# Zero matmuls, half-opened units and a reordered weight split at the start of an encoder layer, and a later place for the sums of w_out

## The chip, the core and the metric

The kernel runs on one core of a Trainium2 chip. The metric is the device time of one execution in microseconds (us). TensorE (PE) multiplies, with its weight loads shown as PEld; VectorE (DVE), ScalarE (ACT) and GpSimd (POOL) do elementwise work, and SyncE (SP) issues nearly all DMAs. Each engine works through its own queue in order and waits on semaphores for the others.

## The reference, cut to what matters

One encoder layer over 1024 tokens of width 1024, in float32:

```python
x = LN0(alpha*x + 0.5*SwiGLU_1(x))        # first feed-forward, width 2816
u = x @ W_in                               # then attention and a two-way SSD scan
x = LN1(alpha*x + concat(a, s) @ W_out)
x = LN2(alpha*x + 0.5*SwiGLU_2(x))        # second feed-forward
x = LN3(alpha*x + sigmoid(x @ W_g + b_g) * (p @ W_p))   # p: 1024 x 256
```

`p @ W_p` (called `e` below) depends on inputs alone, so the kernel computes it first.

## The kernel before, in words

**Products.** A float32 operand is split into a high part that TensorE takes (a cast on ACT, `split_into`) and a low part, the difference (a subtraction on DVE, `lo`, line 87). A product of two such operands is three matmuls per 128 rows of contraction: high with low, low with high, high with high (`mm3`, line 122). One PSUM tile of 128x512 takes one product; the pool `sm` (`pss`) has four such tiles, the pool `big` (`psb`) two of 128x1024.

**The beginning** (`begin`). SP issues the loads of `pT` and `we` (the transposed p and W_p, in eight 256 KB pieces, tiles `xET4h` and `xET4l`), then the identity, the transposed x (`raw`, `wr`, `h`), then the first weights of the feed-forward (`sg`, `xh11`). ACT and DVE split the eight pieces into tiles named `blk`. Sixteen *units* follow (`ple_unit`): each is one 128x512 tile of `e`, with a contraction of 256 rows in two halves, so six matmuls, and ACT copies it out of PSUM (line 632). The list `beside` says which work on x and on the first weights is written between two units: `b11`, `b21` split two quarters of x, `sum1`, `t2`, `sum4` form and split sums of x, and `left(f, i)` splits half `i` of the first weights of row block `f` (`blk<-sg`).

**The first feed-forward.** Each of 22 row blocks `f` takes seven products of twelve matmuls (a Strassen-like scheme): first two that make `sg`, then those with `T2`, `T1`, `T3`, `T4`, `B22` (`ffn_rest`), whose results DVE adds up out of PSUM (`u<-sg,sm` line 378, `u<-u,sm` lines 384 and 387, `sg<-u,sm` line 388) or ACT copies (line 381). The results go to DRAM in `h` and `sg` pieces (line 348, 352).

**The sums of w_out** (`right_sums`, for both feed-forwards). For each of eleven pairs of rows of the second weight, one step issues the stores of the last sums and the loads of the next rows (`wr`, lines 314 and 315) behind SP's queue; the next step forms four sums on DVE (lines 319 to 322). They are needed as weights only in the stage after (`ffn_strassen`, which writes the `big` tiles). `ffn_h` calls one step per row block.

**What sets the order.** PE's order is the order of the program text (`in_order`). In `begin`, ACT and DVE also keep the order of the text. Everywhere else a scheduler places the instructions of ACT, DVE, POOL and SP at build time by its own estimate. `behind(engine)` holds what it encloses behind the last instruction written so far for that engine.

Of the kernel before, what the change touches and what calls it, by code (L numbers as in the profile page):

```python
# [9 lines left out]
F32 = mybir.dt.float32  # L10
F32R = mybir.dt.float32r
BF16 = mybir.dt.bfloat16
# [6 lines left out]
P = 128  # L19
# [17 lines left out]
class Layer:  # L37
# [258 lines left out]
    def right_sums(self, c, i, wo):  # L296

        nc, V = self.nc, self.nc.vector  # L300
        pool = c.enter_context(self.tc.tile_pool(name=f"wsum{i}", bufs=1))
        to = [self.dram.tile([4, P, 512], F32, name=f"wT{i}_{q}") for q in range(NP)]
        lo, hi = slice(0, 512), slice(512, 1024)

        made = []

        def store():
            for dst, src in made:
                nc.sync.dma_start(out=dst, in_=src)
            made.clear()  # L310

        def load(q):
            w1, w2 = (pool.tile([P, D], F32, name=n) for n in ("wr1", "wr2"))
            nc.sync.dma_start(out=w1, in_=wo[2 * q])
            nc.sync.dma_start(out=w2, in_=wo[2 * q + 1])
            return w1, w2, pool.tile([P, 512], F32, name="wt2")

        def sums(q, w1, w2, t):
            V.tensor_tensor(out=w1[:, lo], in0=w1[:, hi], in1=w1[:, lo], op=ALU.subtract)
            V.tensor_tensor(out=t, in0=w2[:, hi], in1=w1[:, lo], op=ALU.subtract)  # L320
            V.tensor_tensor(out=w1[:, hi], in0=w2[:, hi], in1=w1[:, hi], op=ALU.subtract)
            V.tensor_tensor(out=w2[:, lo], in0=w2[:, lo], in1=t, op=ALU.subtract)
            for k, src in enumerate((w1[:, lo], t, w1[:, hi], w2[:, lo])):
                made.append((to[q][k], src))

        tiles = {}

        def step(n):
            q = n // 2
            if n % 2:  # L330
                return sums(q, *tiles[q])
            with self.behind(mybir.EngineType.SP):
                store()
                if q < NP:
                    tiles[q] = load(q)

        return pool, to, [lambda n=n: step(n) for n in range(2 * NP + 1)]

    def left_factors(self, i, tmp):
# [267 lines left out]
    def begin(self, pool, tmp, spare):  # L607


        nc, I = self.nc, self.I  # L610
        V, A = nc.vector, nc.scalar
# [9 lines left out]
        def loaded(src):  # L621
# [2 lines left out]
            todo.append((b, r))  # L624
            return b

        def ple_unit(i, t, n):
            c = slice((t % 4) * P, (t % 4 + 1) * P)
            o = self.pss()
            self.mm3(o, [((pT[t // 4][k][:, 0, c], pT[t // 4][k][:, 1, c]), (we[n][k][:, 0], we[n][k][:, 1])) for k in range(2)])  # L630
            e = kept[i // 4][:, i % 4]
            A.copy(out=e, in_=o)
            with self.behind(mybir.EngineType.SP):
                nc.sync.dma_start(out=self.eD[t][:, n * 512:(n + 1) * 512], in_=e)

        pT, we = [[], []], [[], []]
# [15 lines left out]
        for k in range(4):  # L652
            for src in (I["xT"][:, k], I["xT"][:, k + 4]):
                i = len(raws)
# [13 lines left out]
        u1 = tmp.tile([P, S], F32, name="sg")  # L668
        nc.sync.dma_start(out=u1, in_=I["wi1"][1, 1])
        (r11, r12), (r21, r22) = ([[r[j] for r in raws[i::2]] for j in range(2)] for i in range(2))  # L670
        s = [tmp.tile([P, 512], F32, name=f"s{k + 1}") for k in range(4)]

        for b, r in todo:
            self.split_into(b, r)
# [7 lines left out]
        def put(name, k, src):  # L682
            return lambda: self.put(X, name, k, a, src)

        def less(out, x, y):
            return lambda: V.tensor_tensor(out=out, in0=x, in1=y, op=ALU.subtract)
# [3 lines left out]
        def left(f, i):  # L690
            def do():
                w[f, i] = self.split(sg[f][:, i * 512:(i + 1) * 512])
            return do

        def sum1(k):
            return [less(r11[k], r12[k], r11[k]), less(s[k], r22[k], r11[k])]
# [5 lines left out]
        def b11(k):  # L702
            return [put("B11", k, r11[k])]

        def b21(k):
            return [put("B21", k, r21[k])]

        def t2(k):
            return [put("T2", k, s[k])]

        def sum4(k):
            return [less(r21[k], r21[k], s[k])]


        beside = [[], b11(0) + b21(0), [], b11(1) + b21(1) + sum1(0), [], b11(2) + b21(2) + sum1(1), b11(3) + b21(3) + sum1(2), sum1(3),
                  t2(0) + sum4(0), t2(1) + sum4(1), t2(2) + sum4(2), t2(3) + sum4(3), [left(0, 0), left(0, 1)], [left(1, 0), left(1, 1)], [], []]
        units = [(t, n) for u in range(2) for n in range(2) for t in range(u * 4, u * 4 + 4)]
        for i, ((t, n), work) in enumerate(zip(units, beside)):
            ple_unit(i, t, n)
            for do in work:  # L720
                do()
# [45 lines left out]
        left, sums, g1 = next1  # L767
# [363 lines left out]


    def attention(self, c, mixT, aside, begin):

        nc, tc = self.nc, self.tc
# [89 lines left out]
        for i in range(n + 8):  # L1225
            ps = scores(i) if i < n else None
            los = turn(i - 2) if 2 <= i < n + 2 else []
            if 6 <= i < n + 6:
                values((i - 6) // 4, (i - 6) % 4)
            if (i - 6) % 4 == 1:  # L1230
                normalise()
            if ps is not None:
                softmax(i, ps)
            if i == 1:
                begin()
            for a in los:
                self.lo(*a)
            if i >= 8 and i % 2 == 0 and aside:
                with self.behind(mybir.EngineType.Activation), self.behind(mybir.EngineType.DVE):
                    aside.pop(0)()  # L1240
# [292 lines left out]
    def run(self):  # L1533
# [37 lines left out]
        with ExitStack() as c:  # L1571
            self.in_proj(c, xT)
            rctx.close()
            with self.behind(mybir.EngineType.SP):
                tabs = self.ssd_tables(tables)
            blocks0, aside = [], []

            def begin():
                self.z_last(xT, aside)
                early = [self.ring_raw(I["wm"][k]) for k in range(4)]  # L1580
                aside.extend(tabs)
                aside.extend(lambda i=i, r=r: blocks0.append(self.split(r[:, i * 512:(i + 1) * 512], eng=nc.gpsimd)) for i in range(2) for r in early)

            mixT = [[self.unit(h, 0)] for h in range(2)]
            with ExitStack() as c2:
                self.attention(c2, mixT, aside, begin)
# [396 lines left out]
```

## Time and profile before

| what | value |
|---|---|
| time, median of 3 runs | 1947.11 us (1946.96 to 1948.23) |
| time of the profiled execution | 1948.74 us |
| its span, first to last instruction | 1946.9 us |
| PE busy | 1927.9 us, 99% of the span |
| DVE busy | 1528.0 us, 78% |
| ACT busy | 881.1 us, 45% |
| first matmul starts | 6.75 us |
| the sixteen units end, the first product of the feed-forward starts | 31.25 us |
| first matmul of the stage after the first feed-forward's rows | 450.1 us |

In the lists of instructions, a row gives the start, the time taken, engine, line, operation, what is written and read, and how many equal ones follow each other; in brackets the idle time of the engine before and what ended it. In the list of waits a row gives who waited for whom, the total, how often and the longest. Matmuls overlap, so a matmul's own duration is longer than the distance to the next one.

### The profile page before, as it was taken

The numbers are of one execution on the slowest core, as the hardware profiler recorded it, in microseconds if no ns is written. First come the engines' busy times: TensorE is split into PE (matmuls) and PEld (weight loads), VectorE is DVE, ScalarE is ACT, GpSimd is POOL, SyncE is SP. The second block draws the span as 40 slices with busy tenths as digits, with TensorE's granted clock in tenths as the row PEclk, the third lists the DMA queues.
The fourth block names the chain that finished last, engine by engine and source line by source line (L and its number), as shares of the span: only waits on it lengthen the run. The fifth ranks groups of instructions, "written<-read, shape, count | busy, mean of one in ns | idle before, by whom it ended". The sixth has DMA issues, their size and how long they took to land.

```text
span 1946.9 us, 25645 instructions
## 1 busy us (share of the span) xinstructions
PE 1927.9 (99%) x9132; PEld 1607.8 (83%) x9132; DVE 1528.0 (78%) x2356; ACT 881.1 (45%) x1509; POOL 416.9 (21%) x310
## 2 busy tenths in 40 slices
PE   8999999999999999999999999999999999999998
PEld 6888888888888889888888888888888888888886
DVE  7977777767678668758998878997787787877698
ACT  6433333325444224537887876633333333443311
POOL 0144535430001032001221001013444440001011
PEclk9999999999999999999999999999999999999999
DMA  8434554549866111231002663244545439976022
GB/s 296 143 125 151 190 179 156 190 159 373 297 221 212 63 42 50 84 119 68 7 1 77 212 222 121 90 165 156 190 163 178 173 121 358 331 262 226 32 77 97
DMA packets 147713, 310.34 MB, mean 159 GB/s; under 512 B 18128, under 2 KB 30800, under 8 KB 147584
## 3 DMA queue, kind: packets, MB, share of 16 engines
q1 hardware_dynamic: 147584, 308.69, 45.4%
q8 instruction: 72, 1.18, 0.2%
q14 instruction: 57, 0.47, 0.1%
HBM read 217.21 MB, written 91.42 MB: 159 GB/s over the span
## 4 chain that ended last, share of the span: by engine, by line
PE 94%; DVE 3%; DMA 1%; ACT 1%; issue 1%; POOL 0%; SPq 0%; DVEq 0%; ACTq 0%
PE sm L122 59%; PE big L516 12%; PE sm L516 9%; PE big L122 3%; PE big L1159 3%; PE sm L1181 2%; PE sm L1196 1%; PE sm L1197 1%; DMA yd<-y 1%; DVE nm L1166 1%; DVE conv L977 1%; PE sm L1270 0%; PE big L224 0%; PE sm L224 0%; PE big L909 0%
## 5 line engine op out<-in xcount | busy, mean ns | idle before, releaser
L122 PE MATMUL sm<-xh,blk 128*128 128x512 f32 x1424 | 439.8, 389 | 0.0
L122 PEld LDWEIGHTS sm<-xh,blk 128*128 128x128 f32 x1424 | 267.3, 188 | 55.4
L122 PE MATMUL sm<-xl,blk 128*128 128x512 f32 x736 | 283.8, 389 | 0.0
L122 PE MATMUL sm<-blk,xl 128*128 128x512 f32 (+2 forms) x784 | 238.2, 371 | 0.2 <-ACT xn_t L1010 0.2
L122 PE MATMUL sm<-blk,xh 128*128 128x512 f32 (+2 forms) x584 | 203.3, 379 | 1.6 <-DVE acc L1466 1.1
L108 ACT CAST blk<-raw 128x512 fp32r<-128x512 f32 (+1 forms) x168 | 101.3, 611 | 215.0 <-PE sm L122 134.1
L87 DVE TENSOR_TENSOR blk<-s,blk 128x512 fp32r<-128x512 f32 x176 | 150.8, 861 | 35.2 <-ACT blk L108 33.2
L87 DVE TENSOR_TENSOR blk<-raw,blk 128x512 fp32r<-128x512 f32 (+1 forms) x168 | 146.5, 875 | 40.6 <-ACT blk L108 40.1
L108 ACT CAST blk<-s 128x512 fp32r<-128x512 f32 x172 | 105.7, 622 | 146.5 <-PE sm L122 118.3
L122 PEld LDWEIGHTS sm<-blk,xl 128*128 128x128 f32 x784 | 142.8, 188 | 24.2 <-ACT xn_t L1010 0.5
L122 PEld LDWEIGHTS sm<-xl,blk 128*128 128x128 f32 x736 | 138.2, 188 | 28.6
L178 POOL TENSOR_TENSOR ln_k<-ln_k,mhalf 128x1 f32<-128x1 f32 x32 | 37.4, 1173 | 579.2 <-DVE ln_k L177 563.0
L516 PE MATMUL big<-xh 128*128 128x512 f32 x576 | 138.8, 390 | 0.0
L267 POOL TENSOR_TENSOR s<-raw 128x512 f32<-128x512 f32 x34 | 55.0, 1617 | 387.2 <-DVE blk L87 381.7
L87 DVE TENSOR_TENSOR xh<-blk,xh 128x1024 fp32r<-128x1024 f32 x78 | 95.4, 1223 | 48.4 <-ACT xh L462 42.3
L462 ACT CAST xl<-blk 128x1024 fp32r<-128x1024 f32 x76 | 80.2, 1055 | 113.5 <-PE sm L516 43.7
L462 ACT CAST xh<-blk 128x1024 fp32r<-128x1024 f32 x78 | 82.3, 1055 | 108.1 <-PE big L516 49.9
L122 PEld LDWEIGHTS sm<-blk,xh 128*128 128x128 f32 x584 | 109.9, 188 | 21.3 <-DVE acc L1466 1.4
L516 PEld LDWEIGHTS big<-xh 128*128 128x128 f32 x576 | 107.8, 188 | 22.2
L87 DVE TENSOR_TENSOR xl<-blk,xl 128x1024 fp32r<-128x1024 f32 x76 | 92.7, 1220 | 41.3 <-ACT xl L462 36.7
L516 PE MATMUL big<-xl 128*128 128x512 f32 x480 | 115.8, 390 | 0.0
L122 PE MATMUL sm<-xET2h,blk 128*128 128x512 f32 x352 | 108.4, 389 | 0.0
(343 smaller groups left out, 4018.5 us busy)
## 6 DMA issues: line engine op xcount, KB each, us to landing
raw<-in_wi_dram SPq DMA_DIRECT2D x81, 512.0 KB
blk<-hS SPq DMA_DIRECT2D x154, 256.0 KB
hS<-h SPq DMA_DIRECT2D x88, 256.0 KB
wr<-in_wo_dram SPq DMA_DIRECT2D x44, 512.0 KB
blk<-wT SPq DMA_DIRECT2D x88, 256.0 KB
hS<-sg SPq DMA_DIRECT2D x66, 256.0 KB
wT<-wr SPq DMA_DIRECT2D x66, 256.0 KB
blk<-in_wo_dram SPq DMA_DIRECT2D x66, 256.0 KB
```

Source lines behind the costliest of these rows:

```text
L87: (eng or self.nc.vector).tensor_tensor(out=out, in0=full, in1=hi.bitcast(F32), op=ALU.subtract)
L108: self.nc.scalar.copy(out=b[:, 0, :n], in_=src)
L122: self.nc.tensor.matmul(ps, lhsT=a, rhs=b, start=(i == 0), stop=(i == n - 1))
L178: nc.gpsimd.tensor_tensor(out=r, in0=v, in1=self.mhalf[:, :1], op=ALU.pow)
L267: lambda: G.tensor_tensor(out=s1, in0=a21, in1=a22, op=ALU.add),
L462: A.copy(out=b[:, :, 0], in_=r)
L516: nc.tensor.matmul(ps[q], lhsT=b[:, 0, x, cut], rhs=b[:, 1, y], start=j == i == 0, stop=j == NP - 1 and i == 2)
L977: nc.vector.scalar_tensor_tensor(out=a[:, o], in0=ps[:, o.start + d - c:o.stop + d - c], scalar=cw[:, j, tap:tap + 1], in1=a[:, o], op0=AL ...
L1159: nc.tensor.matmul(ps[:, n * 512:(n + 1) * 512], lhsT=Q[:, h, q0:q0 + P], rhs=K[:, h // 4, j, n * 512:(n + 1) * 512], start=j == 0, stop=j ...
L1166: nc.vector.tensor_reduce(out=nm, in_=ps, axis=AX.X, op=ALU.max, negate=True)
L1181: nc.tensor.transpose(out=pt[:, k], in_=pr[:, kk * P:(kk + 1) * P], identity=self.ident)
L1196: nc.tensor.matmul(po, lhsT=vw, rhs=pth[k // 4][:, k % 4], start=k == 0, stop=False)
```

## The change

At the beginning, DVE fills 256 columns of the tile `s1` with zeros (128x256 float32, read as 512 columns of bf16), and PE runs fourteen matmuls over it into a tile of `big` that nobody reads. Then four units are opened together: of their first half of the contraction (`k = 0`) the high-high terms of all four, then the low-high ones, then the high-low ones. When a unit's turn comes, only its second half is left. The later units run both halves. The three terms now come in another order (high with high first). In `beside`, the split of the first two weight halves moves ahead of the third and fourth `t2`. In the first feed-forward, the four sums of w_out are held behind the last DVE instruction written so far; in the second they stay as they were.

```diff
@@ right_sums, step
             if n % 2:
-                return sums(q, *tiles[q])
+                if i:
+                    return sums(q, *tiles[q])
+                with self.behind(mybir.EngineType.DVE):
+                    return sums(q, *tiles[q])
@@ begin
+        s = [tmp.tile([P, 512], F32, name=f"s{k + 1}") for k in range(4)]
+        V.memset(s[0][:, :256], 0.0)
+        zero, o = s[0].bitcast(BF16), self.psb()[:, :512]
+        for i in range(14):
+            nc.tensor.matmul(o, lhsT=zero[:, :P], rhs=zero[:, :512], start=True, stop=True)
+
+        def ple_part(o, t, n, k, terms):
+            c = slice((t % 4) * P, (t % 4 + 1) * P)
+            for i, j in terms:
+                nc.tensor.matmul(o, lhsT=pT[t // 4][k][:, i, c], rhs=we[n][k][:, j], start=k + i + j == 0, stop=k + i == 2)
+
         def ple_unit(i, t, n):
-            c = slice((t % 4) * P, (t % 4 + 1) * P)
-            o = self.pss()
-            self.mm3(o, [((pT[t // 4][k][:, 0, c], pT[t // 4][k][:, 1, c]), (we[n][k][:, 0], we[n][k][:, 1])) for k in range(2)])
+            o = ahead[i] if i < 4 else self.pss()
+            for k in (0, 1) if i > 3 else (1,):
+                ple_part(o, t, n, k, ((0, 0), (0, 1), (1, 0)))
...
-        s = [tmp.tile([P, 512], F32, name=f"s{k + 1}") for k in range(4)]
...
         beside = [[], b11(0) + b21(0), [], b11(1) + b21(1) + sum1(0), [], b11(2) + b21(2) + sum1(1), b11(3) + b21(3) + sum1(2), sum1(3),
-                  t2(0) + sum4(0), t2(1) + sum4(1), t2(2) + sum4(2), t2(3) + sum4(3), [left(0, 0), left(0, 1)], [left(1, 0), left(1, 1)], [], []]
+                  t2(0) + sum4(0), t2(1) + sum4(1), [left(0, 0), left(0, 1)], t2(2) + sum4(2), t2(3) + sum4(3), [left(1, 0), left(1, 1)], [], []]
         units = [(t, n) for u in range(2) for n in range(2) for t in range(u * 4, u * 4 + 4)]
+        ahead = [self.pss() for t in range(4)]
+        for term in ((0, 0), (1, 0), (0, 1)):
+            for t in range(4):
+                ple_part(ahead[t], t, 0, 0, [term])
```

What stands in the queues. In the rows below, L lines are those of each kernel's own text, and numbers behind tile names only tell buffers apart.

On PE, fourteen pairs of a weight load and a matmul on `s_134`, the zeros, stand ahead of the units' 96 matmuls (`sm<-blk`), which are 96 before and now.

DVE near the end of the units, before: `xET2l<-s` are the low parts of `t2`, `blk<-sg` those of the first weights.

```order
L87 TENSOR_TENSOR xET2l<-s_181,xET2h 128x512
L686 TENSOR_TENSOR raw<-raw,s_181 128x512
L87 TENSOR_TENSOR xET2l<-s_182,xET2h 128x512
L686 TENSOR_TENSOR wr_161<-wr_161,s_182 128x512
L87 TENSOR_TENSOR xET2l<-s_183,xET2h 128x512
L686 TENSOR_TENSOR h_165<-h_165,s_183 128x512
L87 TENSOR_TENSOR blk<-sg,blk 128x512 x4
```

DVE at the same place now:

```order
L87 TENSOR_TENSOR xET2l<-s_135,xET2h 128x512
L699 TENSOR_TENSOR raw<-raw,s_135 128x512
L87 TENSOR_TENSOR blk<-sg,blk 128x512 x2
L87 TENSOR_TENSOR xET2l<-s_136,xET2h 128x512
L699 TENSOR_TENSOR wr_181<-wr_181,s_136 128x512
L87 TENSOR_TENSOR xET2l<-s_137,xET2h 128x512
L699 TENSOR_TENSOR h_185<-h_185,s_137 128x512
L87 TENSOR_TENSOR blk<-sg,blk 128x512 x2
```

The first two weight splits moved four instructions forward.

DVE in a row block of the first feed-forward, before: `wr` and `wt` are the sums of w_out, `u` and `sg` the sums out of PSUM.

```order
L290 TENSOR_TENSOR sg<-sg,sm 128x512
L87 TENSOR_TENSOR blk<-s_2024,blk 128x512
L378 TENSOR_TENSOR u_1890<-sg,sm 128x512
L87 TENSOR_TENSOR blk<-raw,blk 128x512
L87 TENSOR_TENSOR blk<-s_2025,blk 128x512
L319 TENSOR_TENSOR wr_1823<-wr_1823 128x512
L384 TENSOR_TENSOR u_1891<-u_1890,sm 128x512
L87 TENSOR_TENSOR blk<-raw,blk 128x512
L320 TENSOR_TENSOR wt_1827<-wr_1824,wr_1823 128x512
L321 TENSOR_TENSOR wr_1823<-wr_1824,wr_1823 128x512
L322 TENSOR_TENSOR wr_1824<-wr_1824,wt_1827 128x512
```

DVE, the same four sums now (they stand in the next row block):

```order
L290 TENSOR_TENSOR sg<-sg,sm 128x512
L355 TENSOR_TENSOR h_1992<-sg,h_1988 128x512
L319 TENSOR_TENSOR wr_1839<-wr_1839 128x512
L87 TENSOR_TENSOR blk<-s_2193,blk 128x512
L320 TENSOR_TENSOR wt_1843<-wr_1840,wr_1839 128x512
L321 TENSOR_TENSOR wr_1839<-wr_1840,wr_1839 128x512
L381 TENSOR_TENSOR u_2061<-sg,sm 128x512
L322 TENSOR_TENSOR wr_1840<-wr_1840,wt_1843 128x512
```

They moved from behind the block's first sum out of PSUM (line 378, now 381) in one block to ahead of it in the next. The scheduler also reordered DVE, ACT and SP here and there up to the first part of the stage of the `big` tiles; from there to the end of the program every queue stands as before.

## The prediction

> **What bounds the kernel now.** I read the page's busy times and chain first, then PE's waits, then the chain of the first 60 us, then the rows of the stretch that is edited.
>
> ```profile
> span 1946.9 us, 25645 instructions
> PE 1927.9 (99%) x9132; PEld 1607.8 (83%) x9132; DVE 1528.0 (78%) x2356; ACT 881.1 (45%) x1509; POOL 416.9 (21%) x310
> PE 94%; DVE 3%; DMA 1%; ACT 1%; issue 1%; POOL 0%; SPq 0%; DVEq 0%; ACTq 0%
> PE sm L122 <- DVE blk L87: 6.8, 1, 6.8
> PE sm L122 <- DVE acc L1466: 1.1, 1, 1.1
> ```
>
> PE is the bound nearly everywhere. Its one long wait is 6.8 us, for the first split operand; the next is 1.1 us and lies in a part that isn't touched. So what the change can win lies before and inside the units. The chain there:
>
> ```profile
> 0.72 0.40 SPq L623
> 1.17 4.16 DMA xET4h<-in_we_dram
> 5.35 0.63 ACT blk L108
> 6.00 0.70 DVE blk L87
> 6.75 53.44 PE sm L122 x223
> ```
>
> The load of W_p lands at 5.33, ACT's cast is done at 5.98, DVE's low part at 6.70, PE starts at 6.75 and does not stop any more. How fast it runs is the second reading, from PE's rows, windows and groups:
>
> ```profile
> 6.75 24.66 PE L122 MATMUL sm<-blk 128*128 128x512 f32 x96 [6.75 <-DVE blk L87]
> 31.25 0.39 PE L122 MATMUL sm<-xl,blk 128*128 128x512 f32 x1
> 33.97 0.39 PE L122 MATMUL sm<-xl,blk 128*128 128x512 f32 x1
> 6.75:11.95 5.20, 5.20 (x11) 1.00 1.04 371
> 11.95:31.25 19.30, 19.30 (x87) 1.00 1.04 406
> L122 PE MATMUL sm<-blk 128*128 128x512 f32 x11 | 5.4, 654 | 6.8 <-DVE blk L87 6.8
> ...
> L122 PE MATMUL sm<-blk 128*128 128x512 f32 x86 | 19.9, 391 | 0.0
> 9.42 1.05 PE L122 MATMUL sm<-blk 128*128 128x512 f32 x2
> 10.70 1.05 PE L122 MATMUL sm<-blk 128*128 128x512 f32 x2
> 31.25:450.12 418.87, 418.87 (x1849) 1.00 0.48 167
> ```
>
> Between 31.25 and 33.97 lie the twelve matmuls of one product: 0.2267 us each. At that pace 96 take 21.76 us, but the units take 24.50 (6.75 to 31.25). The 2.74 us are lost in the first 5.2 us: there eleven matmuls last 654 ns each, later ones 391. The rows at 9.42 and 10.70 lie three matmuls apart (two in flight span 1.05, one lasts about 0.63): 0.427 each, 1.9 times the later distance. The printed clock column says 1.00 in both windows, so the slow state is read from durations, not from that column. From 31.25 to 450.12 PE is busy in every microsecond: no edit there can win anything, it can only lose.
>
> **The zeros.** DVE starts as the other engines do, at 0.72. No row shows a DVE fill of 128x256; its bounds are the nearest rows:
>
> ```profile
> 0.76 0.10 POOL L1538 MEMSET pad<- 128x8 f32 x1
> 5.15 0.69 DVE L87 TENSOR_TENSOR blk<-xET4h,blk 128x512 fp32r<-128x512 f32 x1 [5.15 <-ACT blk L108]
> ```
>
> Half the columns of the second, 0.35, is my value, so PE starts on zeros at about 1.1 (0.9 to 1.5). If the clock needs PE to be busy for as long as before, 5.2 us, it rises at 6.3. By then 5.2 / 0.427 = 12.2 zeros are done; the other 1.8 take 0.4, at the fast pace. The zeros end at 6.71. They would end at 7.1 if all were slow.
>
> **The units.** The first four real matmuls take high parts only, ready at 5.98; the next four need the low part of `pT` (5.84, from the DVE row above), the last four the low part of `we` (6.70). So from 6.71 PE finds its data. Then 96 x 0.2267 = 21.76, and the first product starts at 28.47 in place of 31.25: **2.78 us won**. Is anything in the way that the old pace hid? ACT's queue, in the order that the change keeps:
>
> ```profile
> 10.95 0.57 ACT L632 COPY xh<-sm 128x512 f32<-128x512 f32 x1
> 13.93 0.59 ACT L632 COPY xh<-sm 128x512 f32<-128x512 f32 x1
> 19.37 0.59 ACT L632 COPY xl<-sm 128x512 f32<-128x512 f32 x1
> 20.37 0.63 ACT L247 CAST xh<-h 128x512 fp32r<-128x512 f32 x1
> ```
>
> The `sm` pool has four tiles, so unit 4 needs unit 0's copy (10.95 to 11.52) and would start at 6.71 + 24 x 0.2267 = 12.15; unit 6 needs unit 2's (done 14.52), starts at 14.87; unit 10 needs unit 6's (19.96), starts at 20.3. Unit 7's copy is behind the casts of x, which wait for DMA and may come no earlier: done by 21.5, and unit 11 starts at 21.67. All hold even if ACT gains nothing, by 0.2 us at the least.
>
> **The first weights.** The first product needs the low part of `w[0, 0]` at about 28.5.
>
> ```profile
> 30.20 2.49 DVE L87 TENSOR_TENSOR blk<-sg,blk 128x512 fp32r<-128x512 f32 x4
> ```
>
> Left behind all `t2` it would be done at 30.9, and PE would wait 2.4 us: without this edit most of the gain would be lost. Moved up by four instructions of 0.6 each, it starts at 27.8 with DVE no earlier, and is done at 28.5; what stands ahead of it on DVE is released by ACT's casts of x, which stand among the units' copies and move up with the units as far as DMA lets them. I cost the edit at 0. The second pair stays at 30.2 to 32.7 at the latest, for a product at 28.47 + 5.44 = 33.9.
>
> **The next pinch, 45 to 60 us.** DVE has hardly a gap there, and the order is new: the sum out of the `T3` product (line 384) now stands ahead of the sum for the next weight and of all four low parts of `B22`.
>
> ```profile
> 47.84 0.69 DVE L763 TENSOR_TENSOR sg<-sg,sm 128x512 f32<-128x512 f32 x1 [0.36 <-PE sm L122]
> ...
> 55.18 0.69 DVE L268 TENSOR_TENSOR s<-s,raw 128x512 f32<-128x512 f32 x1
> 55.79 1.29 DVE L87 TENSOR_TENSOR xl<-raw,xh 128x512 fp32r<-128x512 f32 x2
> 56.99 0.68 DVE L384 TENSOR_TENSOR u<-u,sm 128x512 f32<-128x512 f32 x1
> 58.79 0.69 DVE L87 TENSOR_TENSOR blk<-s,blk 128x512 fp32r<-128x512 f32 x1
> ```
>
> That sum waits until the `T3` product is done. Products follow each other by 2.72 (as above); `T3` is the ninth and ends 24.5 us after the first one's start, at 53.0 now. DVE waits for PE at 47.84, so from there it moves with PE, to 45.06; twelve instructions of 0.605 on, at 52.3, it reaches the sum, waits to 53.2, and then needs seven more instructions at 0.6 until the last low part of `B22`: 57.5. PE takes it as tenth matmul of the next product, at 53.0 + 2.0 + 2.72 = 57.7. So 0.2 us are left. I cost it at 0, and 0.5 at worst.
>
> **The sums of w_out.** DVE's waits in the first feed-forward:
>
> ```profile
> DVE wr L319 <- DMA wr<-in_wo_dram: 18.2, 11, 3.6
> ...
> DVE wt L320 <- DMA wr<-in_wo_dram: 3.6, 6, 1.0
> 209.57 0.68 DVE L322 TENSOR_TENSOR wr<-wr,wt 128x512 f32<-128x512 f32 x1
> ```
>
> DVE waits 21.8 us in all because the sums stand in its queue before their rows have landed. Placed later, that wait goes. But PE lost nothing to it (418.87 of 418.87 busy), so the gain is 0. What it adds: up to four sums (2.4 us) now stand ahead of the sum out of the `T2` product (line 378, now 381). That tile must be free three products later, 8.16 us. Even with the longest wait of before, 3.6 + 2.4 + 0.7 = 6.7. Cost 0. SP's stores of the sums follow at the same place of its queue as before and are needed only after 450 us. From the `big` stage on nothing is reordered: it shifts by what is won.
>
> **Sum.** The profiled execution has 1948.74 us with a span of 1946.9; less 2.78 they would be 1945.96 and 1944.1. The median of the runs is 1.6 below the profiled time; less 2.78 it gives **1944.3**, 0.14% faster. 0.2% (3.9 us) is about what a measurement of this kernel can tell from no change, so my likeliest case counts as the same.
>
> **Rivals.**
> - *The clock rises early* (18 in 100). If a shorter busy stretch is enough, the zeros end before 5.98 and PE waits for data alone: 6.0 + 21.76 = 27.8, 3.48 won, 1943.6. For it: nothing but that one ramp is on record. Against: it took 5.2. In the Trainium skill, "TensorE: Matmul & The Clock Gate" (section "Part 1: The HAM clock gate") says that the clock runs at half until one whole window of about 3.4 us was busy, and that this window is not tied to the kernel's start. By that rule the rise comes 3.4 to 6.8 us after the first zero, an estimate; the trace's 5.2 lies within, and its ratio of 1.9 agrees with half.
> - *Zeros don't wake the clock* (12 in 100). All fourteen run at 0.427 and end at 7.1; the real ones then have 5.2 slow us (12.2 matmuls) and 83.8 x 0.2267 = 19.0 more: 31.3. Nothing is won, 1947.2. Nothing in the trace shows what wakes the clock: the operands' values or the instructions.
> - *VectorE's new order costs PE about 1 us* (7 in 100), between 45 and 110 us where DVE is full: 1945.3.
> - *The sums of w_out stop PE* (4 in 100), the case on the slower side. If the rows land so late that DVE waits over 8.16 - 2.4 - 0.7 = 5.1 us ahead of line 381, PE stops for the rest, once per pair. One instruction's length, 0.6, ten times, makes 6.0: 1944.3 + 6.0 = 1950.3. Against: the longest wait was 3.6 with the sums standing earlier.
>
> **How the numbers follow.** The likeliest case (zeros end between 6.0 and 7.1, 2.0 to 3.4 won) has 59 in 100. The range 1943.1 to 1946.6 holds it, the early clock and VectorE's loss, with some tenths for the runs' own spread; left out are the zeros that don't wake the clock and the stopped PE, 16 in 100. Faster by over 0.2% means under 1943.2: the early clock's best runs only, 0.08. Slower by over 0.2% is the last rival, 0.04. The same: 0.88.
>
> **What would show it.** Right: PE's first matmul at about 1.1; slow matmuls (over 600 ns) among the zeros alone; the first product at about 28.5 with no gap in the units; PE busy without a break until about 447; no DVE wait for `wr`. Wrong: unit matmuls of over 600 ns (the zeros did not help), a gap ahead of the first product (weights late), a gap at 57 to 58 (`B22`), or PE waits in the row blocks (the sums).

## The result, and the profile after

| | before | after |
|---|---|---|
| median, first comparison (22 runs each) | 1948.25 us | 1944.89 us |
| median, a later comparison on one chip (21 and 11 runs) | 1947.83 us | 1945.01 us |
| profiled execution: time, span | 1948.74, 1946.9 us | 1944.84, 1943.0 us |
| first product of the feed-forward starts | 31.25 us | 28.68 us |

The ratio after to before is 0.9985 (95% interval 0.9979 to 0.9990), in the later comparison 0.9985 (0.9976 to 0.9994). The change is 0.15% faster: the intervals exclude 1, and it lies within the 0.2% that the prediction counted as the same. The forecast was 1944.3 us (0.14%).

The page of the changed kernel, first its head, then PE's rows from the start (start, duration, engine, line, operation, count, and in brackets the idle time ahead):

```profile
span 1943.0 us, 25694 instructions
PE 1930.9 (99%) x9146; PEld 1608.2 (83%) x9146; DVE 1521.0 (78%) x2357; ACT 880.9 (45%) x1509; POOL 419.7 (22%) x310
...
1.17 5.87 PE L634 MATMUL big<-s 128*128 128x512 bf16 x14 [1.17 <-DVE s L631]
6.70 22.15 PE L639 MATMUL sm<-blk 128*128 128x512 f32 x96
28.68 0.39 PE L122 MATMUL sm<-xl,blk 128*128 128x512 f32 x1
```

The one 6.8 us wait of PE has become 1.2 us, the zeros run, the units follow without a gap and take 21.98 us (6.70 to 28.68) instead of 24.50. Groups of PE's rows in the first 8 us (count, then busy time and mean ns of one): the slow matmuls are the zeros.

```profile
L634 PE MATMUL big<-s 128*128 128x512 bf16 x14 | 5.9, 609 | 1.2 <-DVE s L631 1.2
L639 PE MATMUL sm<-blk 128*128 128x512 f32 x5 | 1.5, 430 | 0.0
```

The window from the first product to the first `big` matmul, then DVE's waits for the rows of w_out in the first feed-forward (total, times, longest):

```profile
28.68:447.59 418.91, 418.91 (x1849) 1.00 0.48 171
...
DVE wr L319 <- DMA wr<-in_wo_dram: 3.1, 2, 2.5
DVE wt L320 <- DMA wr<-in_wo_dram: 1.1, 2, 0.6
```

PE is busy in all of the 418.91 us, as it was in 418.87 before. DVE's wait fell from 21.8 to 4.2 us, and PE got nothing from it. So 2.57 us were won by 28.68 us, and 2.53 are still there at 447.6. The profiled span is 3.9 us shorter, though. The other 1.3 us come from two later waits of PE, which the prediction did not have: 0.5 us near 1072 us became 0.3, and 1.1 us near 1142 us went. The last group of experiments is about the second.

### The profile page after: what moved, and what is told of

It is laid out like the page before. It is cut to its first block, busy times and chain, and to the rows that moved or that the text cites. A ratio compares the mean times of both kernels' runs of the same rounds, so it can differ in the third digit from the quotient of the medians.

```text
span 1943.0 us, 25694 instructions
## 1 busy us (share of the span) xinstructions
PE 1930.9 (99%) x9146; PEld 1608.2 (83%) x9146; DVE 1521.0 (78%) x2357; ACT 880.9 (45%) x1509; POOL 419.7 (22%) x310
## 4 chain that ended last, share of the span: by engine, by line
PE 95%; DVE 3%; ACT 1%; issue 1%; DMA 0%; POOL 0%; SPq 0%; DVEq 0%; ACTq 0%
PE sm L122 58%; PE big L519 12%; PE sm L519 9%; PE big L122 3%; PE big L1176 3%; PE sm L1198 2%; PE sm L1213 1%; PE sm L1214 1%; PE sm L639 1%; PE sm L1388 1%; PE sm L1287 1%; DVE nm L1183 1%; DVE conv L994 1%; PE sm L1298 0%; PE big L224 0%
## 5 line engine op out<-in xcount | busy, mean ns | idle before, releaser
L87 DVE TENSOR_TENSOR blk<-raw,blk 128x512 fp32r<-128x512 f32 (+1 forms) x168 | 141.1, 843 | 51.8 <-ACT blk L108 51.2
L87 DVE TENSOR_TENSOR blk<-s,blk 128x512 fp32r<-128x512 f32 x176 | 141.8, 809 | 40.6 <-ACT blk L108 38.5
L267 POOL TENSOR_TENSOR s<-raw 128x512 f32<-128x512 f32 x34 | 57.7, 1697 | 381.9 <-DVE blk L87 364.4
```

Of the source, the lines that this page charges most:

```text
L87: (eng or self.nc.vector).tensor_tensor(out=out, in0=full, in1=hi.bitcast(F32), op=ALU.subtract)
L267: lambda: G.tensor_tensor(out=s1, in0=a21, in1=a22, op=ALU.add),
```

## The experiments

Theory A: the slow stretch of TensorE's clock moves from the units to the zeros; the half-opened units and the earlier weight split only keep what that wins; the sums do nothing. Rival B: it is the early opening of the units that wins, and the zeros are not needed. Rival C: the sums' new place shortens the waits near 1072 and 1142 us. Rival D: a pause between zeros and units undoes the zeros.

One variant's ratio to before carries an interval of about 0.09% to each side, 1.75 us. The medians below therefore rank the variants only roughly; the verdicts rest on the rows of the traces.

| kernel | first product, us | median, us | against before in the same runs |
|---|---|---|---|
| no_zeros | 29.86 | 1946.52 | -1.3 |
| zeros_only | 29.43, then a wait | 1946.91 | -0.9 |
| weights_late | 28.30, then a wait | 1947.20 | -0.6 |
| units_whole | 29.22 | 1945.94 | -1.9 |
| sums_early | 28.65 | 1945.63 | -2.2 |
| sums_only | 30.87 | 1948.14 | +0.3 |
| zeros_11 | 28.37 | 1945.12 | -2.7 |
| zeros_6 | 30.70 | 1947.05 | -0.8 |
| zeros_28 | 30.86 | 1948.06 | +0.2 |
| after_again (the changed kernel) | 28.06 | 1945.01 | -2.8 |

### The zeros taken away (no_zeros)

```diff
-        V.memset(s[0][:, :256], 0.0)
-        zero, o = s[0].bitcast(BF16), self.psb()[:, :512]
-        for i in range(14):
-            nc.tensor.matmul(o, lhsT=zero[:, :P], rhs=zero[:, :512], start=True, stop=True)
```

> The changed kernel without its memset and its 14 matmuls over zeros; the half-opened units, the earlier weight split and the place of the sums stay. Theory A (the zeros move TensorE's slow stretch ahead of the units, the other edits only keep that gain): the first unit matmul starts near 6.0 us and runs at the slow spacing (0.42 us apart) to about 11.3; the first product of the weights starts near 30.2 us, 1.5 us later than the 28.68 of the changed kernel, and the whole takes about 1946.4 us where the changed kernel takes 1944.9. Rival B (opening four units on their first half is what wins, the zeros are not needed): first product near 28.7, whole within 0.3 us of the changed kernel. In both, the two later waits near 1070 and 1140 us, which were 1.3 us shorter in the changed kernel's trace, should stand as in that trace if they belong to the edits that stay.

PE's rows, and the group of the unit matmuls up to 9.5 us:

```profile
6.18 23.84 PE L635 MATMUL sm<-blk 128*128 128x512 f32 x96 [6.18 <-ACT blk L108]
29.86 0.39 PE L122 MATMUL sm<-xl,blk 128*128 128x512 f32 x1
...
L635 PE MATMUL sm<-blk 128*128 128x512 f32 x8 | 3.8, 653 | 6.2 <-ACT blk L108 6.2
```

The slow matmuls, 653 ns each, are back among the units, and the first product is 1.2 us later than with the zeros. B falls as it was put: the zeros are needed for the rest of the gain. But the kernel without them is still 1.4 us ahead of before at the first product, so the other edits win something by themselves. The units start at 6.18 instead of 6.75, on ACT's cast and not on DVE's low part. The slow stretch was also shorter than expected, which is no merit of the edits. A row merges many matmuls; their starts one by one, called single starts below, show where the distance falls from 0.427 to 0.227 us. Here that is at 10.14, 3.96 us after the first matmul, against 5.2 us in the first trace of before.

### The zeros alone, on the kernel before (zeros_only)

The edit is the block above, added to the kernel before.

> The kernel before with the memset and the 14 matmuls over zeros alone; units whole, old weight split, old place of the sums. Theory A: no slow matmul among the units; they start near 6.75 us, wait about 0.9 us for the split of a later block, and the low part of the first weights is done near 29.9 us, so the first product starts near 29.9 instead of 31.25: 1.3 us faster than before, about 1.2 us slower than the changed kernel. Rival B: first product near 31.2, whole as before within 0.3 us.

```profile
1.18 5.42 PE L631 MATMUL big<-s 128*128 128x512 bf16 x14 [1.18 <-DVE s L628]
6.86 0.96 PE L122 MATMUL sm<-blk 128*128 128x512 f32 x3 [0.27 <-DVE blk L87]
8.21 21.37 PE L122 MATMUL sm<-blk 128*128 128x512 f32 x93 [0.39 <-DVE blk L87]
29.43 0.39 PE L122 MATMUL sm<-xl,blk 128*128 128x512 f32 x1
30.14 0.73 PE L122 MATMUL sm<-xh,blk 128*128 128x512 f32 x2 [0.33 <-DVE blk L87]
```

As A expected: the units are fast, but PE now runs into DVE three times, twice for low parts of the units and once for the first weights. The second matmul of the first product follows 0.71 us after the first instead of 0.23, so 29.43 counts as 29.9. Zeros alone won about 1.35 us against the first trace of before, half of the change.

### The weight split left late (weights_late)

```diff
-                  t2(0) + sum4(0), t2(1) + sum4(1), [left(0, 0), left(0, 1)], t2(2) + sum4(2), t2(3) + sum4(3), [left(1, 0), left(1, 1)], [], []]
+                  t2(0) + sum4(0), t2(1) + sum4(1), t2(2) + sum4(2), t2(3) + sum4(3), [left(0, 0), left(0, 1)], [left(1, 0), left(1, 1)], [], []]
```

> The changed kernel with the split of the first weights back behind all four t2 sums (one list entry moved). If the place of this split matters: the units end near 28.5 us as in the changed kernel, TensorE then waits for VectorE, and the first product starts between 29.8 us (by the lengths of the VectorE rows of the changed kernel's own trace) and 30.9 us (what the prediction said): 1.1 to 2.2 us slower than the changed kernel. If it does not: first product at 28.7, no difference over 0.3 us.

PE's rows, then DVE's row of the first weights' low parts:

```profile
28.30 0.39 PE L122 MATMUL sm<-xl,blk 128*128 128x512 f32 x1
30.14 0.73 PE L122 MATMUL sm<-xh,blk 128*128 128x512 f32 x2 [1.45 <-DVE blk L87]
...
29.39 1.89 DVE L87 TENSOR_TENSOR blk<-sg,blk 128x512 fp32r<-128x512 f32 x3
```

PE stops for 1.45 us for the first weights, so the edit is needed. The size is the lower one: DVE reaches the split at 29.39, not at 30.20 as in the kernel before, because DVE's queue itself moved up with the units.

### The units whole again (units_whole)

```diff
-            o = ahead[i] if i < 4 else self.pss()
-            for k in (0, 1) if i > 3 else (1,):
+            o = self.pss()
+            for k in (0, 1):
```

The opening loop over `ahead` is left out with it.

> The changed kernel with each of the first eight units computed whole again, zeros kept. Theory A: the first unit needs the second half's split blocks, ready at 7.55 and 8.28 us in the changed kernel's trace, so TensorE idles 0.8 to 0.9 us in all among the first matmuls, and the first product starts near 29.5 us: 0.8 us slower than the changed kernel, 1.7 us faster than before. If the pause of TensorE lets its clock fall back: first product 30.5 or later. If the half-opened units do nothing: 28.7.

```profile
6.75 1.28 PE L639 MATMUL sm<-blk 128*128 128x512 f32 x4
8.22 21.16 PE L639 MATMUL sm<-blk 128*128 128x512 f32 x92 [0.18 <-DVE blk L87]
29.22 0.39 PE L122 MATMUL sm<-xl,blk 128*128 128x512 f32 x1
```

The change opens four units early, not eight as the expectation says. The first product is 0.54 us later than in the changed kernel's first trace (0.8 expected): the fifth matmul waits for a low part of the second half. The pause did not bring the clock down: 92 matmuls take 21.0 us (8.22 to 29.22), 0.228 each.

### The sums, in both directions (sums_early, sums_only)

```diff
-                if i:
-                    return sums(q, *tiles[q])
-                with self.behind(mybir.EngineType.DVE):
-                    return sums(q, *tiles[q])
+                return sums(q, *tiles[q])
```

This is sums_early, on the changed kernel; sums_only is the reverse on the kernel before.

> The changed kernel with w_out's sums back at their old place in VectorE's queue. Theory A (the sums' place costs and gains nothing): the wait of VectorE for the DMA of `wr` is back near 20 us, TensorE is busy without a gap through the first FFN product all the same, and the time is that of the changed kernel within 0.5 us. Rival C (the sums' new place is what shortened the waits of TensorE near 1070 and 1140 us): the 0.9 to 1.1 us gap near 1142 us is there, and the whole is about 1.3 us slower than the changed kernel.

> The kernel before with the sums behind VectorE's queue, and nothing else of the change. Theory A: first product at 30.5 to 31.5 us as before, no VectorE wait of 18 us for `wr`, time as before within 0.5 us. Rival C: the gap near 1142 us is gone and the whole is 1.3 us faster than before.

sums_early, DVE's wait and PE's first product; then sums_only, PE's rows:

```profile
DVE wr L319 <- DMA wr<-in_wo_dram: 20.9, 10, 4.1
...
28.65 0.39 PE L122 MATMUL sm<-xl,blk 128*128 128x512 f32 x1
```

```profile
6.90 24.13 PE L122 MATMUL sm<-blk 128*128 128x512 f32 x96 [6.90 <-DVE blk L87]
30.87 0.39 PE L122 MATMUL sm<-xl,blk 128*128 128x512 f32 x1
```

With the wait of 20.9 us back, the first product stands where it stood, and PE has no gap of over 0.25 us between it and the `big` stage. In sums_only the edit alone leaves the time as it was before (ratio 0.9999, interval 0.9990 to 1.0008). sums_early's median is 0.7 us above the changed kernel's, inside the intervals (its ratio to before is 0.9988, 0.9979 to 0.9997).

### How many zeros (zeros_11, zeros_6, zeros_28)

Each changes only the 14 of the loop.

> The changed kernel with 11 matmuls over zeros in place of 14. By the five traces so far TensorE's slow stretch lasts 3.9 to 5.5 us from its first matmul. 11 slow ones end at 1.17 + 11 x 0.427 = 5.87 us, the blocks of the first unit are ready near 6.0 to 6.2 us. Theory A: TensorE starts the units near 6.1 us, with at most 2 slow matmuls among them, first product at 28.0 to 28.5 us, time 0 to 0.6 us better than the changed kernel's. Rival D (a pause of 0.1 to 0.3 us between zeros and units starts the slow stretch anew): slow unit matmuls to 9.5 us or later, first product at 29.5 us or later, 0.8 to 2 us slower than the changed kernel.

```profile
1.17 4.88 PE L634 MATMUL big<-s 128*128 128x512 bf16 x11 [1.17 <-DVE s L631]
6.21 22.32 PE L639 MATMUL sm<-blk 128*128 128x512 f32 x96 [0.16 <-ACT blk L108]
28.37 0.39 PE L122 MATMUL sm<-xl,blk 128*128 128x512 f32 x1
```

A pause of 0.16 us between zeros and units did no harm: one slow unit matmul, then the fast pace from 6.8 us. D falls for pauses of this size. The median, 1945.12 us, is not to be told from 14 zeros.

> The changed kernel with 6 matmuls over zeros: they end near 1.17 + 6 x 0.427 = 3.73 us, and TensorE stands idle for some 2.4 us until the first blocks are ready. If the clock rises a fixed time after the first matmul, whatever follows (3.9 to 5.5 us in the traces): units fast from the start, first product near 28.1 us, as with 11. If TensorE has to be busy without a break: the slow stretch starts again with the units, 3.9 to 5.5 us long, so they run slow to 10 or 11.7 us, first product at 29.7 to 30.6 us, time like that of the changed kernel without zeros (1946.5).

```profile
1.17 2.74 PE L634 MATMUL big<-s 128*128 128x512 bf16 x6 [1.17 <-DVE s L631]
6.31 24.55 PE L639 MATMUL sm<-blk 128*128 128x512 f32 x96 [2.40 <-ACT blk L108]
30.70 0.39 PE L122 MATMUL sm<-xl,blk 128*128 128x512 f32 x1
```

Six zeros and a pause of 2.4 us win nothing on the clock. The units run at the slow pace again, by the single starts until 11.60, 5.3 us after the first of them. So it is not a fixed time after the first matmul that counts. In the Trainium skill, "TensorE: Matmul & The Clock Gate" (section "Part 1: The HAM clock gate") asks for one whole busy window of about 3.4 us. The six zeros are busy for 2.74, and the trace agrees. What lost the effect, the short burst or the pause behind it, this run can't tell apart: no run has a long burst with a long pause.

> The changed kernel with 28 matmuls over zeros in place of 14. TensorE works its queue in order, so zeros beyond the end of the slow stretch hold the units back at full speed: 9 to 13 slow ones to 5.1 to 6.7 us, the other 15 to 19 at 0.217 us each, so the units start near 9.4 to 10.0 us and the first product near 31.3 to 31.8 us: as before, 2.7 to 3.1 us slower than with 14. If the surplus is hidden behind the loads: 28.7.

```profile
1.17 8.04 PE L634 MATMUL big<-s 128*128 128x512 bf16 x28 [1.17 <-DVE s L631]
8.86 22.16 PE L639 MATMUL sm<-blk 128*128 128x512 f32 x96
30.86 0.39 PE L122 MATMUL sm<-xl,blk 128*128 128x512 f32 x1
```

Surplus zeros are paid in full: PE's queue is in order, the units start 2.16 us later than with 14 and end 2.18 us later. By the single starts the clock rose at 4.95 us in this execution, after nine slow zeros where the 14 had thirteen; the rest ran 0.216 us apart. Fourteen more at 0.216 are 3.02 us, and four fewer slow zeros save 0.84: 2.18. Nine slow zeros lie inside the expected 9 to 13, so the expected 31.3 to 31.8 us was itself too late: from 4.95, 19 zeros at 0.216 and 96 matmuls at 0.2267 give 30.8.

### The same kernels again (after_again, after_third, before_again)

> The changed kernel once more. The gap of TensorE near 1142 us was under 0.25 us in its first trace, and 0.35 to 1.15 us in most of the others. If it belongs to the edits of the change, it is missing again; if it goes with how the DMAs of y, raw and bc fall in one execution, it comes out anywhere from 0 to 1.15 us. The time is 1944.5 to 1945.5 us either way, the first product at 28.0 to 29.3 us by the length of the slow stretch (3.4 to 6.8 us).

> The changed kernel a third time, one look for the same gap: 0 if it belongs to the change, anywhere from 0 to 1.15 us if it goes with the execution.

> The kernel before once more, one look: the gap near 1143 us was 1.15 us in its first trace. If it belongs to the old order it is 1.1 to 1.2 us again; if it goes with the execution, it comes out anywhere from 0 to 1.15 us. The slow stretch of TensorE was 5.2 us there; by the traces so far it comes out anywhere from 3.9 to 5.5 us.

PE's first rows of after_again, then of after_third:

```profile
1.17 5.18 PE L634 MATMUL big<-s 128*128 128x512 bf16 x14 [1.17 <-DVE s L631]
6.01 22.21 PE L639 MATMUL sm<-blk 128*128 128x512 f32 x96
28.06 0.39 PE L122 MATMUL sm<-xl,blk 128*128 128x512 f32 x1
```

```profile
1.17 6.12 PE L634 MATMUL big<-s 128*128 128x512 bf16 x14 [1.17 <-DVE s L631]
6.77 22.31 PE L639 MATMUL sm<-blk 128*128 128x512 f32 x96
28.92 0.39 PE L122 MATMUL sm<-xl,blk 128*128 128x512 f32 x1
```

The same instructions start their first product at 28.06, 28.68 or 28.92 us. before_again has it at 31.36. after_third and before_again were one execution each, of 1946.15 and 1949.01 us. Now the late wait, in PE's waits between 1130 and 1150 us: before_again, sums_early, after_again, after_third, one row each (total, times, longest).

```profile
PE sm L122 <- DVE acc L1466: 1.2, 1, 1.2
```

```profile
PE sm L122 <- DVE acc L1480: 1.1, 1, 1.1
```

```profile
PE sm L122 <- DVE acc L1483: 0.4, 1, 0.4
```

```profile
PE sm L122 <- DVE acc L1483: 1.1, 1, 1.1
```

The changed kernel's first trace has no such row in this window. One and the same kernel shows 0, 0.4 and 1.1 us, so the 1.1 us that its first profile won there are no sure property of the change. What differs is a DMA in the chain that ends at this wait, in the first trace and in the third (start, duration):

```profile
1127.42 4.16 DMA raw<-in_wm_dram
```

```profile
1128.65 4.84 DMA raw<-in_wm_dram
```

It lands at 1131.58 and at 1133.49, 1.9 us later, though the start of the third ran only 0.24 us behind. C is not needed for the spread. It isn't ruled out for the mean: the four traces with the sums at their old place have 1.0 to 1.2 us, the ten with the new place 0 to 1.1, on average 0.6. So at most about 0.5 us could be the sums' doing. sums_only has 0.4 us in its trace, as C would have it, but its time did not fall (+0.3 us where C asked for 1.3 less). This stays open within the 1.75 us of the intervals.

## Why the prediction was right

- **What bounds.** The first 5.2 us held what could be won, as the prediction said, but it put all of the 2.74 us down to the slow clock and said that PE does not stop after 6.75. PE did stop, as its weight loads in the trace of before show:

```profile
8.40 0.93 PEld L122 LDWEIGHTS sm<-blk 128*128 128x128 f32 x3 [0.72 <-DVE blk L87]
```

  The fourth weight load waits for a low part of the second half. Matmul durations overlap, so the row of the matmuls hid it. By the single starts, eleven distances of 0.427 in place of 0.2267 make 2.2 us of the 2.74, the longer first distance 0.17, and the two distances around the stop 0.37. The zeros take the first part away, the half-opened units the stop. In all 2.57 us were won.
- **The zeros.** DVE began the fill at 0.84, 0.12 us later than taken, and needed 0.27 us, 0.08 less than the estimate from half of a 128x512 row. The two nearly cancel, and PE began at 1.17 (1.1 forecast). Zeros do wake the clock: in zeros_28 they run 0.216 us apart from 4.95 us on, before any other matmul. The units' row begins at 6.70, and 6.71 was forecast, but this agreement is luck. The last zero and the first two unit matmuls:

```profile
6.67 0.38 PE L634 MATMUL big<-s 128*128 128x512 bf16 x1
6.70 0.58 PE L639 MATMUL sm<-blk 128*128 128x512 f32 x1
...
7.11 0.39 PE L639 MATMUL sm<-blk 128*128 128x512 f32 x1
```

  The second unit matmul starts 0.44 us after the last zero, which is one zero's distance and one unit's (0.216 + 0.2267). So the first one's start is recorded early, and the zeros' time is up near 6.89, 0.18 us later than forecast. The step that failed is the one that took 5.2 us for a constant. By the single starts, the slow stretch lasted 3.8 us (zeros_28) to about 6.0 (after_third) in the fourteen traces, 5.2 and 5.4 in the two of before, and 5.5, 4.2 and 6.0 in three of the changed kernel. That the first profile drew 5.5, close to 5.2, is luck too. So "the clock rises early", with 18 in 100, is no rival mechanism but one end of the same spread: after_again comes closest to it, with its first product at 28.06 where the rival said 27.8. The estimate of 3.4 to 6.8 us that the prediction drew from the Trainium skill ("TensorE: Matmul & The Clock Gate", section "Part 1: The HAM clock gate") holds in all fourteen.
- **The units.** 96 x 0.2267 = 21.76 was forecast; from the row's start to the first product 21.98, 22.05 and 22.15 were measured. Counted from 6.89, where the zeros' time is up, it is 21.79 in the first trace: the pace was right, and the 0.2 us missing from the forecast 2.78 are the later end of the zeros. No unit waited for ACT in that trace. In after_again, the earliest one, a weight load of the units waited 0.19 us for ACT's copy at 21.10 and cost 0.04 us: the margin of 0.2 us that the prediction left for unit 11 was just used up.
- **The first weights.** The split was forecast to be done at 28.5; DVE's row below ends at 28.12, 0.6 us ahead of need. Cost 0 was right, but "PE would wait 2.4 us" without the edit was mis-sized: 1.45 us. The term left DVE at its old times, and DVE had moved up by 0.8.
- **The pinch at 45 to 60 us.** DVE's rows, then PE's for the tenth matmul of that product:

```profile
26.84 1.28 DVE L87 TENSOR_TENSOR blk<-sg,blk 128x512 fp32r<-128x512 f32 x2
...
53.37 0.69 DVE L387 TENSOR_TENSOR u<-u,sm 128x512 f32<-128x512 f32 x1 [0.78 <-PE sm L122]
56.98 0.68 DVE L87 TENSOR_TENSOR xl<-h,xh 128x512 fp32r<-128x512 f32 x1
...
57.93 0.39 PE L122 MATMUL sm<-xl,blk 128*128 128x512 f32 x1
```

  DVE waits for `T3` until 53.37 (53.2 forecast), the last low part is done at 57.66 (57.5), PE takes it at 57.93 (57.7). The slack of 0.2 us was real, 0.27, and it held.
- **The sums of w_out.** Gain 0, cost 0: the wait went and came back with sums_early, and PE was busy throughout either way.
- **The sum.** 2.78 us won were forecast; the later comparison of medians has 2.82 (1947.83 less 1945.01), the first 3.36, the first products of the traces 2.57. One pair of traces is a draw: the two of before and the three of the changed kernel average 31.3 and 28.55, 2.75 apart. The forecast's base was the median of three runs, 1947.11; in larger counts before's median was 1947.83 and 1948.25. In the first comparison the base came out 1.1 us higher and the gain 0.6 larger than forecast, and the two errors partly cancel: 1944.89 is only 0.6 above 1944.3.

Taken together: each of the three edits at the start, taken away by itself, leaves the first product (with the wait behind it) at 29.2 to 29.9 us, and the zeros alone reach 29.9. Neither part does it alone. The zeros alone win about half, since DVE then takes the rest back. The other edits without the zeros win 1.4 us in no_zeros, of which about 0.6 is that execution's short slow stretch (an estimate: 1.24 us shorter, at 1 - 0.2267/0.427 = 0.47 us each), so about 0.8 is theirs. The remaining gain needs both, so theory A's "only keep what that wins" is too strong.

## What to carry to other kernels

When the first real operand arrives late, fill the wait with matmuls over zeros on a tile that nobody reads. Size them to end about when the data is ready: six, with a pause of 2.4 us behind them, won nothing on the clock, eleven with a pause of 0.16 us did as well as fourteen, and each one too many costs its full 0.216 us. Then look at what the slow start had hidden, since the engines that split the first operands become the next wait. Before crediting an edit with a late gap that vanished, profile the unchanged kernel again.

## What the runs showed of the hardware

- The length of the slow stretch is a draw per execution, 3.8 to 6.0 us here, and moves the start of an unchanged kernel by up to 0.9 us (28.06 to 28.92).
- The first float32 matmul behind the bf16 zeros is recorded only 0.03 us after the last zero, and the next one 0.41 to 0.43 us later. Where the clock is already up this is no lost time: in zeros_28 the last zero starts at 8.83 and the second unit matmul at 9.29, 0.46 us for two distances of 0.216 and 0.2267. A stretch that begins at such a row looks about 0.2 us too long.
- At the fast clock a bf16 matmul of 128x512 takes 0.216 us to the next and a float32 one 0.2267; at the slow clock both take 0.427.
